# Scores of the sample tokens with the cached keys, computed during the projection of q, k, v; the norm's last addition on VectorE

## The chip, the core and the metric

The kernel runs on one core of a Trainium2 chip. The metric is the device time of one execution in microseconds. Three executions of the kernel before took 2411.53, 2411.56 and 2414.08 us; the median is 2411.56 us. One more execution was profiled, and all rows in this document's part on the kernel before come from it.

## What is computed

One decoder layer, in float32. A prompt of 4096 rows and 32 sample rows (8 sequences of 4 new tokens) go through one input projection [q | k | v | gate | lru | gate], then dilated window attention and a gated recurrence, then one output projection with a layer norm. Cut to what the change touches:

```python
q2, k2, v2, ga2, xl2, gl2 = _project(x_s, w_in)          # 32 sample rows
k_all = jnp.concatenate([ck, kh2], axis=1)               # 2048 cached keys of each sequence, and 4 new ones
v_all = jnp.concatenate([cv, vh2], axis=1)
# patterns (128,1), (512,4), (2048,16): 129 keys each, backwards from the query with stride d
idx = w_buf + jnp.arange(t)[:, None] - d * jnp.arange(N_DIL_KEYS + 1)[None, :]
s = jnp.einsum('bqhd,bqjhd->bhqj', q, jnp.take(k_all, idx, axis=1)) * (q.shape[-1] ** -0.5)
# softmax of each pattern, values, the three patterns merged by their denominators
...
z = ALPHA * x + mixed @ w_out
zn = (z - z.mean(-1)) * rsqrt(z.var(-1) + LN_EPS)
return zn * ln_g + ln_b                                  # prompt and sample rows
```

## The kernel before

Every engine runs its instructions in the order in which the program issues them, and so does SyncE's queue (SP), which issues nearly all DMAs: an instruction that waits holds up all that stand behind it on its engine.

**Phase 1** projects q, k and v. The prompt is cut into 8 tiles of 512 rows, t = 0 to 7. For t from 1 to 6 the loop runs four q groups (`qk_groups(t, 0)`), four k groups (`qk_groups(t, 1)`) and then the v stage (`v_groups(t)`); I call this a sweep. A q or k group is 24 matmuls into one PSUM bank; ScalarE copies the bank (L202) and VectorE subtracts that copy from it (L203), and SP stores both. There are six banks, used in turn (`pp`). The v stage is 8 steps (`chunk`), each of 12 matmuls, into four banks. Between its steps it prepares the input of the next sweep, one of 8 chunks per step (`next_chunk`, `prep_chunk`): VectorE transposes (L110), ScalarE rounds (L113), VectorE subtracts (L114: both inputs lie in SBUF), SP stores to DRAM. At its end SP issues the 2 MB load of the tile after next (`next_x`, L104), and the four banks are copied to `vt` tiles, of which there are three (`evac_v`, L208, two on VectorE, two on ScalarE), and stored. `sample_rows` projects the sample's v and writes the sample's q to DRAM (`qsd`); before, it stands behind the sweep t = 1.

**Phases 2 and 3** (prompt attention; recurrence and gates) aren't touched.

**Phase 4** is the output projection, in 33 blocks of 48 matmuls. A plan of times, `at(tick, f)`, sets the order: block b of the prompt starts at tick 8 b, and what belongs to it follows at fixed distances: `norm1` (VectorE, residual and statistics, L1340 to L1346; frees the block's two banks), `norm2` (VectorE, L1353), `norm3` (ScalarE, L1359), `norm4` (GpSimd, adds ln_b, L1367), `store`. `mix_split` (L1274 on ScalarE, L1275 on VectorE with two SBUF inputs) makes the left operands of the blocks to come. The sample's attention is planned into the same ticks. For each of 8 sequences: `row_q` loads its q, copied to all 128 partitions (1 MB); for each of the three patterns p = 2, 0, 1 `fetch` loads keys (256 KB for p = 2, 1 MB for the others), `k_mul` multiplies them by q on GpSimd (L1435), `k_sum` sums over the 64 columns of a head on VectorE (L1439). After four sequences `soft1` to `soft6` make the softmax, and `v_mm` multiplies with cached values on TensorE (L1492).

## Time and profile before

| | |
|---|---|
| median of three executions | 2411.56 us |
| profiled execution | 2415.58 us, span 2413.9 us (1.7 us lie around the span) |
| TensorE busy, share of the span | 93% |
| VectorE, ScalarE, GpSimd | 58%, 46%, 29% |
| sweeps t = 1 to 3 of phase 1 | about 107 to 305 us of the span |
| phase 4 | from about 1938 us to the end |
| granted TensorE clock, mean | 0.966 of full speed |

The profile gives for each engine the time in which it was busy, cuts the span into 40 slices, and names for each wait the instruction that ended it. A name such as `po<-S,mx` is output<-inputs, and L1286 is the line of the kernel.

### The profile page before, as it was taken

What the parts mean: (1) busy time and instruction counts of PE and PEld (TensorE: products, weight loads), DVE (VectorE), ACT (ScalarE), POOL (GpSimd) and SP (SyncE); (2) the same over time, 40 slices, a digit from 0 to 9 for tenths busy, and PEclk for the clock granted to TensorE, in tenths of its full rate; (3) what the DMA queues carried; (4) which work ended last, traced back from release to release, by engine and by line L of the source; (5) the groups of instructions that cost most, each with busy time, mean ns of one, the idle gap of its engine ahead of it and who ended that gap; (6) DMA issues with size and microseconds to landing.
All of it is one profiled execution on the core that took longest, in us unless ns stands there. A gap on an engine that the chain in (4) does not pass through costs nothing. (4 is left out here: it accounts for less than half of the span.)

```text
span 2413.9 us, 42627 instructions
## 1 busy us (share of the span) xinstructions
PE 2251.9 (93%) x15274; PEld 1896.7 (79%) x15274; DVE 1406.4 (58%) x3489; ACT 1099.5 (46%) x2819; POOL 695.2 (29%) x522
## 2 busy tenths in 40 slices
PE   6999999997999899989988988799999989989998
PEld 5878888886788778868777877799999967657776
DVE  4423222232476757546665655577878779998544
ACT  3212122222566566646655654566777741222221
POOL 1000000000445546464636465000000026646111
PEclk9999999998999999989999999899999989989999
DMA  6854556649666867777696755455545556668551
GB/s 174 261 189 151 173 175 200 209 186 245 181 165 174 206 155 178 182 182 172 160 211 168 182 142 134 139 174 156 168 156 178 187 183 227 244 224 325 200 187 57
DMA packets 324946, 444.18 MB, mean 184 GB/s; under 512 B 58628, under 2 KB 193412, under 8 KB 319616
## 3 DMA queue, kind: packets, MB, share of 16 engines
q1 hardware_dynamic: 324576, 440.94, 61.8%
q8 instruction: 122, 2.00, 0.4%
q14 instruction: 88, 0.72, 0.1%
q0 software_dynamic: 160, 0.52, 0.1%
HBM read 305.79 MB, written 135.60 MB: 183 GB/s over the span
## 5 line engine op out<-in xcount | busy, mean ns | idle before, releaser
L465 POOL CAST qg<-S 128x512 fp32r<-128x512 f32 x256 | 274.7, 1101 | 620.1 <-DMA S<-qd 489.7
L1286 PE MATMUL po<-S,mx 128*128 128x512 f32 x1536 | 379.9, 407 | 22.6 <-DVE xr L1340 16.8
L1286 PEld LDWEIGHTS po<-S,mx 128*128 128x128 f32 x1536 | 294.7, 194 | 113.8 <-issue 26.9
L522 DVE CUSTOM_DVE_ANT_0 sm<-s,mask 128x256 f32<-128x256 f32 (+1 forms) x768 | 270.7, 390 | 154.9 <-PE s L516 108.4
L526 ACT ACTIVATE sm<-sm,st 128x256 f32<-128x256 f32 (+1 forms) x512 | 252.9, 495 | 160.2 <-DVE st L522 133.9
L535 PE MATMUL pt<-ident,sm 128*128 128x128 f32 x1368 | 238.9, 292 | 9.4 <-ACT sm L526 9.2
L551 PE MATMUL o<-pts,v 128*64 128x128 f32 x2736 | 239.8, 292 | 6.6 <-DMA v<-vd 3.7
L539 DVE COPY pts<-pt 128x512 f32<-128x512 f32 x228 | 157.4, 690 | 142.3 <-PE pt L535 111.7
L515 PE MATMUL s<-S,qg 128*128 128x256 f32 x512 | 160.8, 334 | 51.4 <-POOL qg L465 51.0
L535 PEld LDWEIGHTS pt<-ident,sm 128*128 128x128 f32 x1368 | 145.3, 143 | 78.4 <-issue 55.3
L551 PEld LDWEIGHTS o<-pts,v 128*64 128x64 f32 x2736 | 144.7, 138 | 61.9 <-issue 4.6
L203 DVE TENSOR_TENSOR stg<-pp,stg 128x512 fp32r<-128x512 f32 x56 | 51.1, 916 | 239.0 <-ACT stg L202 239.0
L188 PE MATMUL pp<-S,xh 128*128 128x512 f32 x768 | 178.8, 393 | 6.3 <-ACT S L127 5.2
L314 PE MATMUL pp<-xh,S 128*128 128x512 f32 x448 | 176.0, 393 | 0.0
L315 PE MATMUL pp<-xh,S 128*128 128x512 f32 x448 | 174.5, 390 | 0.8 <-POOL xh L114 0.8
L188 PEld LDWEIGHTS pp<-S,xh 128*128 128x128 f32 x768 | 145.1, 189 | 38.4 <-ACT S L127 6.1
L316 PE MATMUL pp<-xh,S 128*128 128x512 f32 x448 | 174.6, 390 | 0.0
L526 ACT ACTIVATE sm<-sm,ac 128x128 f32<-128x128 f32 (+1 forms) x256 | 114.8, 450 | 103.8 <-DVE ac L522 103.2
L139 PE MATMUL xl<-xh,S 128*128 128x256 f32 x512 | 147.9, 289 | 5.0 <-DMA xh<-xtd 3.3
L653 PE MATMUL f<-xh,S 128*128 128x256 f32 x512 | 148.2, 289 | 2.6 <-DMA xh<-xtd 2.6
L143 PE MATMUL xl<-xh,S 128*128 128x256 f32 x512 | 148.2, 289 | 1.9 <-POOL S L128 1.4
L656 PE MATMUL f<-xh,S 128*128 128x256 f32 x512 | 148.2, 289 | 0.0
(287 smaller groups left out, 5303.9 us busy)
## 6 DMA issues: line engine op xcount, KB each, us to landing
xh<-xtd SPq DMA_DIRECT2D x256, 256.0 KB, 5.5
S<-qd SPq DMA_DIRECT2D x128, 256.0 KB, 5.0
xtd<-xh SPq DMA_DIRECT2D x56, 512.0 KB, 2.6
gb<-wd SPq DMA_DIRECT2D x64, 384.0 KB, 5.8
v<-vd SPq DMA_DIRECT2D x264, 64.0 KB, 4.3
S<-kd SPq DMA_DIRECT2D x64, 256.0 KB, 7.1
xr<-in_x_prompt_dram SPq DMA_DIRECT2D x32, 512.0 KB, 4.9
arena<-in_cache_k_dram SPq DMA_DIRECT2D x16, 1024.0 KB, 8.3
```

The source lines that it names most:

```text
L188: nc.tensor.matmul(p, l, m, start=(c == 0 and a + b == 0), stop=(c == 7 and (a, b) == ((1, 0) if j < 2 else (0, 1))))
L314: nc.tensor.matmul(ps, wh, xh, start=(c == 0), stop=False)
L315: nc.tensor.matmul(ps, wh, xl, start=False, stop=False)
L316: nc.tensor.matmul(ps, wl, xh, start=False, stop=(c == 7))
L465: nc.gpsimd.tensor_copy(o, q.bitcast(F32))
L515: nc.tensor.matmul(s[:, h], q_ap(x, h, 0), k, start=True, stop=False)
L522: nc.vector.tensor_tensor_reduce(x.sm[:, h, o], s[:, h, i], self.mask[:, x.pat, o], -0.125, 3e38, ALU.add, ALU.min, x.stat[:, h, 0:1])
L526: nc.scalar.activation(x.sm[:, h, o], x.sm[:, h, o], AF.Exp, bias=x.stat[:, h, 0:1], scale=-1.0, accum_out=x.stat[:, h, 1:2])
L535: nc.tensor.transpose(p[:, h, kb], x.sm[:, h, kb * 128:(kb + 1) * 128], self.ident)
L539: e(x.pt, p)
L551: nc.tensor.matmul(o[h * 64:(h + 1) * 64, x.b * 128:(x.b + 1) * 128], v[:, h * 64:(h + 1) * 64], x.pt[:, h, kb], start=(kb == kbs[0]), sto ...
L1286: self.nc.tensor.matmul(ps[j], l, self.Wo[j][c][:, s], start=(c == 0 and s == 0 and l is mh), stop=(c == 7 and l is ml))
```

## The change

Multiplications and sums of the keys are taken out of phase 4 and put into the sweeps t = 1 to 3 of phase 1. A counter of steps (`decode_step`) is called before each q and k group and after every second step of the v stage, 12 times in a sweep. A score product starts every 1.5 steps: load, multiplication one step later, sum two steps later, store of the sums to DRAM (`scd`) three steps later. The key tile `dk` is one of two buffers (pool `kfp`); the 256 KB tiles of p = 2 take a `vt` tile; q has one buffer. `sample_rows` moves ahead of t = 1. In phase 4 `scores_in` loads the sums (three DMAs of 128 KB), the softmax of the two groups stands at ticks 12 and 120, and `norm4` is on VectorE for all blocks.

```diff
+        self.scd = dr.tile([3, 128, 2 * 4 * NS], F32, name="scd")
+        dqp = xctx.enter_context(tc.tile_pool(name="p1d", bufs=1))
@@ v_groups
                 next_chunk(t, c)
+                if c % 2:
+                    decode_step()
@@ phase1
+        def row_q(b):
+            D["q"] = dqp.tile([128, NT, DA], F32, tag="q", name="qb")
+            nc.sync.dma_start(out=D["q"].rearrange("p t d -> p (t d)"),
+                              in_=dap(self.qsd, b * NT * DA, [[0, 128], [1, NT * DA]]))
+        def dec_load(b, p):
+            o = kfp.tile([128, NT, DA], F32, tag="kf", name="dk")
+            if p == 2:
+                k = sp.tile([128, DA], F32, tag="vt", name="dk2")
+                nc.sync.dma_start(out=k, in_=dap(I["cache_k"], b * 2048 * DA + 1920 * DA, [[DA, 128], [1, DA]]))
+            else:
+                a, n = ((0, 16), (1536, NT))[p]
+                k = o
+                nc.sync.dma_start(out=o, in_=dap(I["cache_k"], b * 2048 * DA + a * DA, [[n * DA, 128], [1, NT * DA]]))
+            D[b, p] = k, o
+        def dec_mul(b, p):
+            k, o = D[b, p]
+            nc.gpsimd.tensor_mul(o, k[:, None, :].to_broadcast([128, NT, DA]) if p == 2 else o, D["q"])
+        def dec_sum(b, p):
+            o = D.pop((b, p))[1]
+            D["s", b, p] = r = dqp.tile([128, NS], F32, tag="sc", name="sc", bufs=4)
+            nc.vector.tensor_reduce(r, o.rearrange("p t (h d) -> p (t h) d", d=HD), op=ALU.add, axis=AX.X)
+        def dec_save(b, p):
+            nc.sync.dma_start(out=self.scd[p, :, b * NS:(b + 1) * NS], in_=D.pop(("s", b, p)))
+        uses = [(b, p) for b in range(8) for p in (2, 0, 1)]
+        for n, (b, p) in enumerate(uses):
+            g = 1.5 * n
+            if p == 2:
+                decode.setdefault(int(g + (0.5 if b else 0)), []).append((row_q, b))
+            decode.setdefault(int(g), []).append((dec_load, b, p))
+            decode.setdefault(int(g + 1), []).append((dec_mul, b, p))
+            decode.setdefault(int(g + 2), []).append((dec_sum, b, p))
+            decode.setdefault(int(g + 3), []).append((dec_save, b, p))
+        order = {dec_sum: 0, row_q: 1, dec_load: 2, dec_mul: 3, dec_save: 4}
 ...
         def qk_groups(t, j, kp, each=None):
             for m in range(4):
+                decode_step()
                 qk_group(t, j, m)
+        sample_rows()
         for t in range(1, n_t - 1):
 ...
-            if t == 1:
-                sample_rows()
@@ phase4
         def norm4(b):
-            e = nc.gpsimd if b < n_b - 1 else nc.vector
             for w in parts(b):
-                e.tensor_add(L[b][:, w], L[b][:, w], lnb[:L[b].shape[0], w])
+                nc.vector.tensor_add(L[b][:, w], L[b][:, w], lnb[:L[b].shape[0], w])
+        def scores_in():
+            for p in range(3):
+                nc.sync.dma_start(out=SC[p].rearrange("p a b s -> p (a b s)"), in_=self.scd[p])
 ...
-        at(-17.5, row_q, 0)
+        at(-17.5, scores_in)
 ...
-    k.k_start, k.k_step, k.v_step = k.soft[9], k.soft[10], k.soft[11:]
+    k.soft_at, k.v_step = (12.0, 120.0), (24.0, 22.0)
```

VectorE's order in phase 1 from the end of the v stage t = 1 to the last k group of t = 2, before (`vt` are the copies of v, `so` those of `sample_rows`, `stg` the subtractions of the q and k groups):

```order
L208 COPY vt<-pp 128x512 x2
L349 COPY so<-pp 32x512 x2
L203 TENSOR_TENSOR stg<-pp,stg 128x512 x4
L203 TENSOR_TENSOR stg<-pp,stg 128x32x16 x4
L110 STREAM_TRANSPOSE raw<-X 128x512
```

and with the change (`sc<-dk` are the sums):

```order
L210 COPY vt<-pp 128x512 x2
L382 TENSOR_REDUCE sc<-dk 128x32
L205 TENSOR_TENSOR stg<-pp,stg 128x512 x2
L382 TENSOR_REDUCE sc<-dk 128x32
L205 TENSOR_TENSOR stg<-pp,stg 128x512
L382 TENSOR_REDUCE sc<-dk 128x32
L205 TENSOR_TENSOR stg<-pp,stg 128x512
L205 TENSOR_TENSOR stg<-pp,stg 128x32x16
L382 TENSOR_REDUCE sc<-dk 128x32
L205 TENSOR_TENSOR stg<-pp,stg 128x32x16
L382 TENSOR_REDUCE sc<-dk 128x32
L205 TENSOR_TENSOR stg<-pp,stg 128x32x16 x2
```

Between the subtractions that free the banks now stand five sums, each of which waits for GpSimd's multiplication.

SP's order at the same place, before (`X` is the 2 MB load, `vd` the store of v, `qd` that of q):

```order
L104 DMA X<-in_x_prompt_dram 32x16x256 x4
L210 DMA vd<-vt 128x512 x4
L343 DMA out_dram<-vs 32x512
L350 DMA qsd<-so 32x512
L350 DMA out_dram<-so 32x512
L192 DMA qd<-stg 128x2x512 x4
```

and with the change (`dk` are the loads of keys, `qb` that of a sequence's q, `scd` the stores of sums):

```order
L105 DMA X<-in_x_prompt_dram 32x16x256 x4
L212 DMA vd<-vt 128x512 x4
L372 DMA dk<-in_cache_k_dram 128x2048
L385 DMA scd<-sc 128x32
L194 DMA qd<-stg 128x2x512
L368 DMA dk_1561<-in_cache_k_dram 128x512
L385 DMA scd<-sc 128x32
L194 DMA qd<-stg 128x2x512
L361 DMA qb<-qsd 128x2048
L194 DMA qd<-stg 128x2x512
L372 DMA dk<-in_cache_k_dram 128x2048
L385 DMA scd<-sc 128x32
```

The loads of keys and of q now stand behind the stores of v, one by one between the stores of q.

VectorE's order in the v stage t = 2, before (`raw` and `xh` are the preparation of a chunk):

```order
L110 STREAM_TRANSPOSE raw<-X 128x512
L114 TENSOR_TENSOR xh<-raw,xh 128x2x256
L110 STREAM_TRANSPOSE raw<-X 128x512
L114 TENSOR_TENSOR xh<-raw,xh 128x2x256
L110 STREAM_TRANSPOSE raw<-X 128x512
```

and with the change:

```order
L111 STREAM_TRANSPOSE raw<-X 128x512
L115 TENSOR_TENSOR xh<-raw,xh 128x2x256
L111 STREAM_TRANSPOSE raw<-X 128x512
L115 TENSOR_TENSOR xh<-raw,xh 128x2x256
L382 TENSOR_REDUCE sc<-dk 128x32
L111 STREAM_TRANSPOSE raw<-X 128x512
```

A sum stands behind the second, the fourth and the eighth chunk.

## Rows read from the trace of the kernel before

**Rows 1.** The page: busy time of TensorE (us, share of the span, instructions), and the busy tenths of VectorE and GpSimd in 40 slices of 60 us.

```profile
PE 2251.9 (93%) x15274; PEld 1896.7 (79%) x15274; DVE 1406.4 (58%) x3489; ACT 1099.5 (46%) x2819; POOL 695.2 (29%) x522
...
DVE  4423222232476757546665655577878779998544
...
POOL 1000000000445546464636465000000026646111
```

**Rows 2.** Busy time by stretch: the early and the late part of phase 4. Columns: stretch, its length, busy us and instructions of each engine, granted clock, share of the DMA engines, GB/s.

```profile
1967.60:2160.00 192.40, 162.01 (x653) 121.54 (x654) 182.91 (x188) 40.01 (x87) 110.82 (x31) 0.91 0.62 229
2160.00:2405.80 245.80, 244.29 (x1186) 174.56 (x1185) 142.11 (x240) 51.28 (x108) 76.33 (x25) 1.00 0.56 207
```

**Rows 3.** Groups of VectorE's instructions from 1967 to 2160 us: busy us, mean ns of one, and idle time before them.

```profile
L1275 DVE SCALAR_TENSOR_TENSOR mx<-B,mx 128x256 fp32r<-128x256 f32 x28 | 42.6, 1580 | 2.1 <-ACT mx L1274 2.1
L1275 DVE SCALAR_TENSOR_TENSOR mx<-A,mx 128x256 fp32r<-128x256 f32 x26 | 40.3, 1607 | 9.4 <-ACT mx L1274 9.4
L1439 DVE TENSOR_REDUCE SC<-arena 128x32 f32<-128x2048 f32 x16 | 36.1, 2258 | 0.0
...
L1340 DVE SCALAR_TENSOR_TENSOR xr<-xr,po 128x512 f32<-128x512 f32 x28 | 17.8, 674 | 0.0
L1353 DVE SCALAR_TENSOR_TENSOR xr<-xr,mv,lng 128x1024 f32<-128x1024 f32 x13 | 16.4, 1261 | 0.0
```

**Rows 4.** The order in time of VectorE and of GpSimd around 2016 us (start, us, instruction, count).

```profile
2016.23 10.41 DVE L1275 SCALAR_TENSOR_TENSOR mx<-A,mx 128x256 fp32r<-128x256 f32 x4 [0.73 <-ACT mx L1274]
...
2016.49 9.53 POOL L1435 TENSOR_TENSOR arena<-arena,qb 128x2048 f32<-128x2048 f32 x2
```

**Rows 5.** The same line L1275 from 2000 to 2150 us, by the tile it writes: shortest, median and longest in ns.

```profile
L1275 DVE SCALAR_TENSOR_TENSOR mx<-B,mx x23: 410/416/4836, 2005.8 to 2148.4; 128x256 fp32r<-128x256 f32 x23
L1275 DVE SCALAR_TENSOR_TENSOR mx<-A,mx x20: 402/414/4835, 2016.2 to 2135.9; 128x256 fp32r<-128x256 f32 x20
```

**Rows 6.** The chain that ended last, late in phase 4: half the value products of a sequence, and a block.

```profile
2274.85 1.83 PE do L1492 x16
2276.68 11.44 PE po L1286 x48
```

**Rows 7.** TensorE's largest group from 1967.6 to 2160 us.

```profile
L1286 PE MATMUL po<-S,mx 128*128 128x512 f32 x606 | 154.5, 415 | 18.3 <-DVE xr L1340 16.2 <-DVE mx L1275 1.8
```

**Rows 8.** The order in time at the beginning of phase 4: TensorE's blocks 2 and 3 with the wait ahead of each, and ScalarE's work that stands ahead of the first.

```profile
1972.42 13.61 PE L1286 MATMUL po<-S,mx 128*128 128x512 f32 x48 [4.90 <-DVE xr L1340]
1988.79 1.56 PE L1286 MATMUL po<-S,mx 128*128 128x512 f32 x4 [2.76 <-DVE xr L1340]
...
1970.47 0.72 ACT L1274 ACTIVATE mx<-A 128x256 fp32r<-128x256 f32 x2 [10.45 <-DMA hd<-sg]
```

**Rows 9.** The granted clock (third number from the end) behind the first of these waits.

```profile
1972.00:1976.00 4.00, 3.58 (x8) 2.77 (x9) 3.29 (x9) 1.65 (x6) 0.34 (x1) 0.50 1.00 382
```

**Rows 10.** The multiplication (L1435) and the norm's last addition (L1367), over the whole span: shortest, median and longest in ns.

```profile
L1435 POOL TENSOR_TENSOR arena<-arena,qb x16: 4567/4774/5570, 1980.5 to 2217.9; 128x2048 f32<-128x2048 f32 x16
...
L1367 POOL TENSOR_TENSOR xr<-xr,lnb x31: 2337/2398/2412, 1989.4 to 2388.2; 128x1024 f32<-128x1024 f32 x31
...
L1367 DVE TENSOR_TENSOR xr<-xr,lnb x3: 692/693/1211, 2399.2 to 2410.1; 128x512 f32<-128x512 f32 x2, 32x1024 f32<-32x1024 f32 x1
```

**Rows 11.** Busy time by stretch in phase 1: the first groups of t = 1, the eight q and k groups of t = 2, its v stage. Columns as in rows 2.

```profile
101.10:107.50 6.40, 5.56 (x25) 4.17 (x24) 3.92 (x6) 2.33 (x4) 2.56 (x2) 1.00 0.97 394
...
174.20:217.90 43.70, 43.70 (x196) 36.17 (x194) 7.40 (x9) 6.62 (x9) 0.00 (x0) 1.00 0.44 137
217.90:239.80 21.90, 21.90 (x98) 18.16 (x97) 12.88 (x19) 6.69 (x10) 0.00 (x0) 1.00 0.50 201
```

**Rows 12.** VectorE and ScalarE in the v stage t = 2, in order of time: the last k group's subtraction, then the preparation of the first chunk, the start of the second, and the end of the eighth.

```profile
219.24 1.15 DVE L203 TENSOR_TENSOR stg<-pp,stg 128x512 fp32r<-128x512 f32 x1 [4.29 <-ACT stg L202]
220.30 0.70 DVE L110 STREAM_TRANSPOSE raw<-X 128x512 f32<-128x512 f32 x1
221.75 0.69 DVE L114 TENSOR_TENSOR xh<-raw,xh 128x512 fp32r<-128x512 f32 x1 [0.75 <-ACT xh L113]
222.36 0.70 DVE L110 STREAM_TRANSPOSE raw<-X 128x512 f32<-128x512 f32 x1
...
237.80 0.69 DVE L114 TENSOR_TENSOR xh<-raw,xh 128x512 fp32r<-128x512 f32 x1 [1.41 <-ACT xh L113]
```

**Rows 13.** Behind a v stage: SP's load of the next tile and stores of v (start, time from the first to the last), and the copy of the fourth bank behind the v stage t = 1 with its wait.

```profile
238.89 2.61 SPq L104 DMA_DIRECT2D X<-in_x_prompt_dram  x4
241.60 12.34 SPq L210 DMA_DIRECT2D vd<-vt  x4
...
182.09 0.59 ACT L208 COPY vt<-pp 128x512 f32<-128x512 f32 x1 [14.73 <-DMA vd<-vt]
```

**Rows 14.** The one place in phase 1 where GpSimd and VectorE work side by side, at the end of t = 0.

```profile
99.49 1.29 POOL L114 TENSOR_TENSOR xh<-raw,xh 128x512 fp32r<-128x512 f32 x1 [2.04 <-ACT xh L113]
...
100.03 1.29 DVE L114 TENSOR_TENSOR xh<-raw,xh 128x512 fp32r<-128x512 f32 x1 [0.82 <-ACT xh L113]
```

**Rows 15.** A 1 MB load with nothing of weight behind it: its issue by SP.

```profile
2326.83 0.38 SPq L1426 DMA_DIRECT2D arena<-in_cache_v_dram  x1
```

**Rows 16.** The stretches behind that issue (the share of the DMA engines is the number before the last).

```profile
2328.00:2332.00 4.00, 4.00 (x26) 1.86 (x25) 2.40 (x4) 0.00 (x0) 0.00 (x0) 1.00 0.90 313
2332.00:2336.00 4.00, 4.00 (x19) 3.22 (x18) 3.79 (x10) 1.53 (x5) 0.00 (x0) 1.00 0.02 6
```

More of the change, by code (lines that the diff above doesn't have):

```diff
@@ L350, in sample_rows, with decode_step @@
                 nc.sync.dma_start(out=dst, in_=o)
+        D, decode = {}, {}
+        def row_q(b):
[31 more added lines that the diff above has]
+        order = {dec_sum: 0, row_q: 1, dec_load: 2, dec_mul: 3, dec_save: 4}
+        tick = [0]
+        def decode_step():
+            for f, *a in sorted(decode.pop(tick[0], []), key=lambda v: order[v[0]]):
+                f(*a)
+            tick[0] += 1
         def qk_groups(t, j, kp, each=None):
             for m in range(4):
+                decode_step()
                 qk_group(t, j, m)
@@ L1377, in norm @@
                 at(t + d, f, b)
-        ck, cv = I["cache_k"], I["cache_v"]
+        cv = I["cache_v"]
         CB = 2048 * DA
@@ L1426, in fetch @@
                 nc.sync.dma_start(out=arena[s], in_=dap(src, b * CB + a * DA, [[k * DA, 128], [1, NT * DA]]))
-        def row_q(b):
-            D["q"] = qp.tile([128, NT, DA], F32, tag="X", name="qb")
-            nc.sync.dma_start(out=D["q"].rearrange("p t d -> p (t d)"),
-                              in_=dap(self.qsd, b * NT * DA, [[0, 128], [1, NT * DA]]))
-        def k_mul(n, p, s):
-            k, o, q = D.pop(n), arena[s], D["q"]
-            nc.gpsimd.tensor_mul(o, k[:, None, :].to_broadcast([128, NT, DA]) if p == 2 else o, q)
-        def k_sum(b, p, s):
-            o, sc = arena[s], SC[p][:, b // 4, b % 4]
-            nc.vector.tensor_reduce(sc, o.rearrange("p t (h d) -> p (t h) d", d=HD), op=ALU.add, axis=AX.X)
         def soft1(G):
@@ L1566, in phase4 @@
         for G in range(2):
+            for i, f in enumerate((soft1, soft2, soft3, soft4, soft5, soft6)):
+                at(self.soft_at[G] + self.soft[i], f, G)
             for i in range(4):
[L1568 to L1579 removed]
+                t0 = self.soft_at[G] + self.soft[6] + self.v_step[G] * i
                 for k, p in enumerate((2, 0, 1)):
@@ L1583, in phase4 @@
         for t, kind, b, p in sorted(uses):
-            if kind == "k" or p < 2:
+            s = None
+            if p < 2:
                 s = n % 4
```

46 lines of the change are left out of this document (14 added, 32 removed).

## The prediction

> **What bounds the kernel now.** I read the page first. TensorE is busy for 93% of the span, so only time in which it waits or runs at a low clock can be won; VectorE's slices show a 9 around 2000 us, and GpSimd is nearly empty in phase 1 [rows 1]. So I read the busy time by stretch. Early in phase 4, from 1967.6 to 2160 us, VectorE is busy for 182.9 of 192.4 us and TensorE for 162.0 at a granted clock of 0.91; later TensorE is full at 1.00 [rows 2]. The early stretch is VectorE's. Its groups say why: the 54 subtractions of L1275 take 82.9 us, 1.6 us each, and the sums 36.1 [rows 3]. In order of time four such subtractions take 10.41 us while GpSimd multiplies for 9.53 [rows 4], and by tile their median is 0.41 us and their longest 4.84 [rows 5]: most are undisturbed, some wait out a whole multiplication.
>
> In phase 1 it is the other way round: in the sweep t = 2 TensorE is busy for all of the 43.7 us of q and k groups and all of the 21.9 us of the v stage, VectorE for 7.4 and 12.9, GpSimd for nothing [rows 11]. A free engine is not yet a free place; that depends on what stands behind the moved instructions.
>
> **What phase 4 gives back.** Undisturbed, a block takes 11.44 us for 48 matmuls, 0.2383 each, and half a sequence's value products 1.83 [rows 6]. The early stretch holds 606 such matmuls [rows 7], 144.4 us, and 47 other products [rows 2]: 32 value products at 3.7 and 15 small ones, say 2. That makes 150 of 192.4 us, so 42 are lost. Not all comes back. Block 2 waits 4.90 us, and that wait goes back over VectorE to ScalarE's copies, which wait for the store of phase 3's last result [rows 8]; behind it the clock is 0.50 for 4 us, which costs 2 more [rows 9]. Block 3 waits 2.76 us, behind the first block's norm and a set of small tables on VectorE [rows 8], and again some 2 at half clock. I leave about 10 of these there and take 32 as the gain; bounds 24 (a new wait of the same kind) and 38 (both waits shrink).
>
> Does VectorE still hold TensorE up? Taken from its 182.9 us are the sums, 36.1, and the excess of 54 subtractions over 0.42, 60 [rows 3, 5]; added are 14 additions at 2 x 0.69 [rows 10], 19 us, and up to 1.2 us of waiting for ScalarE ahead of each, 17. That is 123 us in 150: hidden. Where this cover is gone an addition costs its 1.4 us per block. GpSimd's 2.40 us additions end [rows 10].
>
> The sample's 24 matmuls and transposes move ahead of t = 1, where TensorE now waits 6.40 - 5.56 = 0.84 us for the last chunks [rows 11]; they cover that: -0.9.
>
> **What phase 1 pays.** 24 multiplications of 4.77 us on GpSimd [rows 10] and 24 sums of 2.26 on VectorE [rows 3] go into three sweeps of 65.6 us. By load alone both fit: 38 us of 65.6 on GpSimd, 20.3 + 18.1 on VectorE. But the loads, the q buffer and the in-order queues form a chain, and VectorE's sums stand in it ahead of the subtractions that free TensorE's banks and ahead of the preparation of the next tile. I walk the sweep t = 2.
>
> A 1 MB load takes 4.8 us: issued at 2326.83, the DMA engines are idle from about 2331.6 [rows 15, 16]. Behind the v stage SP issues the 2 MB of the tile after next and then the stores of v; the fourth waits until ScalarE finds one of three `vt` tiles free, 14.73 us [rows 13]. Nothing was harmed by that before. Now the load of the keys of product 8 stands behind it. So from the end of the v stage: hold 14.7; load 4.8; multiplication 4.8; only now is the q buffer free, next q 4.8; multiplication 9, 4.8; sum 9, 2.3; the subtraction of one q group and its store, which stand ahead of the next load, 1.2; load 11, whose buffer sum 9 has freed, 4.8; multiplication 4.8; sum 2.3; the last two k groups' subtractions, 2 x 1.15 [rows 12]. Sum 51.6 us until VectorE starts on the next tile. Before, it starts 43.7 + 2.4 after the v stage [rows 11, 12], 46.1. It is 5.5 late, and the six banks are about used up by then.
>
> Then the v stage. A chunk takes VectorE 2.06 us from transposition to transposition [rows 12], eight 16.5; three sums add 6.8; and the subtraction of L114 has two SBUF inputs, as L1275 has. Beside a GpSimd instruction it took 1.29 us instead of 0.69 and ended with that instruction [rows 14]. A multiplication met in this stage costs 4.77 less what transposition and rounding cover, 1.4: 3.4. By the order of the loads two fall into the stage in the first two sweeps and three in the third, 23.5 in all. The q and k groups' subtractions read PSUM and one SBUF tile, as L1340, which stays at 0.67 beside the multiplications [rows 3]; I charge them nothing.
>
> The Trainium skill, "SBUF — State Buffer", section "Who interferes with whom", has it that the engine that starts first keeps the shared port for its whole instruction and the other "fully blocks", and that tensor_reduce never contends. By that rule the meetings cost the 23.5 just taken. Read as a proportional slowing instead, from the mean of 1.59 us against 0.42 [rows 3, 5], each of 24 subtractions would grow by 1.9 us, 46 in all, and the forecast by 22. The median beside the longest [rows 5] agrees with the rule; the sums stay at 2.26 us [rows 3].
>
> Three sweeps: 3 x (51.6 + 16.5 + 6.8) + 23.5 = 248 us, where 3 x 65.6 = 197 are there: 51 late. At the end of a v stage there is slack: the eighth chunk is ready at 238.5 [rows 12], and TensorE, done at 239.8, comes to it after seven chunks of three matmuls, 4.8 us later: 6.1. So TensorE loses 45. Bounds: 22, if no subtraction is held up (51 - 23.5 - 6), and 65, if loads take 7 us, as three of them stand in each sweep's chain.
>
> **The sum.** 45 - 32 - 0.9 = +12 us. On the profiled execution's 2415.6 that is 2428; that execution is 4 us above the median, so 2424 for a median. This measurement tells a change from none at about 0.2%, 5 us.
>
> **Rivals.**
> 1. *All of phase 1 is hidden.* For it: six banks take 27 us of lateness from the q and k groups, and TensorE is the only bound there. Then 2411.6 - 33 = 2379. It decides if a sweep's chain falls from 51.6 to below 46 and the v stage to below 24.3 (18.2 and the slack); without the hold of 14.7 it would nearly. Chance 0.08.
> 2. *Only the v stage pays.* The q and k groups stay in time, the v stage takes 16.5 + 6.8 + 6.8 = 30.1 against 24.3 twice, and 33.5 once: 21 us. 21 - 33 = -12, 2400: faster. It decides if the hold is at most 9 us, since then VectorE starts in time. Chance 0.20.
> 3. *The loads are late too.* The moved transfers are 26 MB in 197 us; at the 382 GB/s that full DMA engines moved [rows 9] that is 68 us, a share of 0.35, on top of 0.44 and 0.50 [rows 11]. If loads take 8 us because they meet stores and the tile load, 3 sweeps x 3 loads x 3.2 = 29 more: 2453. Chance 0.11.
> 4. *Phase 4 gives back only 20*, because `norm4` waits for ScalarE ahead of the norm that frees the banks: 2436. Against it stands the room of 27 us above. Chance 0.06.
>
> The forecast itself has 0.55. The range of 2394 to 2452 holds it, the fourth rival, most of the second and about half of the third. Its own range is 2412 to 2442. Faster by over 0.2%: all of the first, 0.16 of the second and 0.02 of the forecast's lower end, 0.26. Within 0.2%: 0.09. Slower: 0.65.
>
> **What would show it.** In the changed profile the v stages t = 1, 2, 3 should end late by about 15 us more each time; TensorE should wait for VectorE's L115 at the start of the q groups of t = 2, 3, 4, and for a bank ahead of the v stages; VectorE should wait for GpSimd's multiplication at L382, and some subtractions of L115 should take up to 5 us. SP should stand for some 14 us behind each tile load, the keys behind it. In phase 4 L1327 should be at 0.42 us throughout, and TensorE without waits behind block 3. Wrong would be the forecast if the sums find their products ready (then the first or second rival), or if TensorE still waits in phase 4.

## The result, and the profile after

The changed kernel takes **2439.44 us** (median of 4 runs, 2435.91 to 2444.75), against 2411.55 for the kernel before on the same chip: a ratio of 1.0115, 95% interval 1.0095 to 1.0135. It is slower by 27.9 us, where I had forecast 12. The sign is as forecast and the time lies within the range, but the size is more than twice the forecast's.

The profiled execution took 2439.8 us (span 2438.1), 24.2 more than that of before. From its page, as in [rows 1], with the granted clock by slices of 61 us in addition:

```profile
PE 2259.7 (93%) x15274; PEld 1891.3 (78%) x15274; DVE 1387.9 (57%) x3520; ACT 1094.5 (45%) x2819; POOL 618.8 (25%) x491
...
DVE  4354653222257666664755566467888786455555
...
POOL 1044350000145464745544566300000000000000
PEclk9998889999899999999999999799999998999999
```

GpSimd's work has moved from the end to the third to sixth slice, and from the fourth to the sixth the clock is down as well. The windows tell what each stretch gained or lost (length, busy us and instructions of each engine, clock, DMA share, GB/s): phase 1; phases 2 and 3; phase 4. First before, then after.

```profile
0.00:573.60 573.60, 552.15 (x2591) 459.10 (x2592) 179.71 (x278) 136.12 (x214) 13.57 (x21) 0.99 0.60 194
573.60:1937.60 1364.00, 1267.22 (x10746) 1121.11 (x10745) 875.13 (x2737) 854.65 (x2378) 489.61 (x430) 0.96 0.65 172
1937.60:2413.90 476.30, 432.54 (x1942) 316.53 (x1940) 351.59 (x477) 108.73 (x228) 192.04 (x71) 0.95 0.57 208
```

```profile
0.00:632.60 632.60, 577.67 (x2591) 467.16 (x2592) 258.33 (x302) 135.79 (x215) 124.09 (x45) 0.95 0.68 220
632.60:1986.30 1353.70, 1258.05 (x10747) 1112.96 (x10745) 876.51 (x2734) 849.96 (x2376) 489.66 (x430) 0.97 0.65 173
1986.30:2438.10 451.80, 423.94 (x1942) 311.22 (x1940) 253.05 (x485) 108.74 (x229) 5.01 (x16) 0.97 0.45 159
```

Phase 1 lost **59.0 us** (forecast: 45 - 0.9), phase 4 gave back **24.5** (forecast: 32). Phases 2 and 3, which the change does not touch, are 10.3 us shorter in this execution: the same matmuls (10746 and 10747 in the rows) were busy for 9.2 us less, at a clock of 0.97 and not 0.96. In the profiled executions of the experiments that stretch takes 1354 to 1365 us, so I count it as variation between executions. 59.0 - 24.5 - 10.3 is the 24.2 of the two profiled executions; without the 10.3 it would be 34.5, where the medians are 27.9 apart. No run assigns that rest.

Of phase 1's 59.0 us TensorE waited 33.5 more, and 25.5 are the same 2591 matmuls taking longer at the lower clock.

**Phase 1, sweep t = 2.** The same places as in [rows 12, 13]: SP's queue, then GpSimd, then VectorE (start, duration, instruction, wait ahead of it).

```profile
194.37 2.60 SPq L105 DMA_DIRECT2D X<-in_x_prompt_dram  x4
197.07 13.15 SPq L212 DMA_DIRECT2D vd<-vt  x4
210.31 0.38 SPq L372 DMA_DIRECT2D dk<-in_cache_k_dram  x1
...
221.10 0.32 SPq L361 DMA_DIRECT2D qb<-qsd  x1
...
233.90 0.41 SPq L372 DMA_DIRECT2D dk<-in_cache_k_dram  x1
...
216.47 4.61 POOL L377 TENSOR_TENSOR dk<-dk,qb 128x2048 f32<-128x2048 f32 x1 [23.05 <-DMA dk<-in_cache_k_dram]
225.88 4.60 POOL L377 TENSOR_TENSOR dk<-dk,qb 128x2048 f32<-128x2048 f32 x1 [4.80 <-DMA qb<-qsd]
...
240.57 4.57 POOL L377 TENSOR_TENSOR dk<-dk,qb 128x2048 f32<-128x2048 f32 x1 [3.51 <-DMA dk<-in_cache_k_dram]
...
210.39 1.29 DVE L205 TENSOR_TENSOR stg<-pp,stg 128x512 fp32r<-128x512 f32 x2 [10.84 <-ACT stg L204]
...
249.48 0.70 DVE L111 STREAM_TRANSPOSE raw<-X 128x512 f32<-128x512 f32 x1
```

From the issue of the tile's load at 194.37 to VectorE's first transposition at 249.48 the chain takes 55.1 us. In brackets stands what I had put: hold (from the issue of the tile's load until the stores of v are out of SP's queue and the first load of keys is issued) 15.9 (14.7), load 6.2 (4.8), multiplication 4.6 (4.8), row of q 4.8 (4.8), multiplication 4.6 (4.8), sum, subtraction and store 3.4 (3.5), load 6.7 (4.8), multiplication 4.6 (4.8), sum and two subtractions 4.3 (4.6). The order was right; both loads were longer. The first row of VectorE shows that the hold has a second way: ScalarE, too, waits for a store of v, and VectorE behind ScalarE.

Then the v stage: three subtractions of L115 that met a multiplication, the multiplications beside them, and the undisturbed subtraction of the eighth chunk.

```profile
250.86 4.71 DVE L115 TENSOR_TENSOR xh<-raw,xh 128x512 fp32r<-128x512 f32 x1 [0.69 <-ACT xh L114]
256.93 4.85 DVE L115 TENSOR_TENSOR xh<-raw,xh 128x512 fp32r<-128x512 f32 x1 [0.73 <-ACT xh L114]
275.99 3.92 DVE L115 TENSOR_TENSOR xh<-raw,xh 128x512 fp32r<-128x512 f32 x1 [0.73 <-ACT xh L114]
281.26 0.69 DVE L115 TENSOR_TENSOR xh<-raw,xh 128x512 fp32r<-128x512 f32 x1 [0.73 <-ACT xh L114]
...
250.43 4.60 POOL L377 TENSOR_TENSOR dk<-dk,qb 128x2048 f32<-128x2048 f32 x1 [5.28 <-DMA dk<-in_cache_k_dram]
256.63 4.61 POOL L377 TENSOR_TENSOR dk<-dk,qb 128x2048 f32<-128x2048 f32 x1 [1.60 <-DMA dk<-in_cache_k_dram]
274.85 4.52 POOL L377 TENSOR_TENSOR dk<-dk,qb 128x2048 f32<-128x2048 f32 x1 [13.61 <-DMA dk<-in_cache_k_dram]
```

Each of the three ends 0.54 us after the multiplication that it met. They cost 4.0 + 4.2 + 3.2 = 11.4 us; I had put two at 3.4. I had read [rows 14] as a subtraction that ends with GpSimd's instruction; its rows, too, put the end 0.54 us later (101.32 against 100.78). The waits between 95 and 420 us (engine, line, what it waited for; us in total, times, longest) name the same links:

```profile
POOL dk L377 <- DMA dk<-in_cache_k_dram: 120.2, 17, 23.0
...
DVE sc L382 <- POOL dk L377: 77.5, 14, 10.6
...
ACT vt L210 <- DMA vd<-vt: 54.2, 3, 19.8
```

and TensorE's groups on the page show at which places this reached it (busy us, mean ns, idle before):

```profile
L190 PE MATMUL pp<-S,xh 128*128 128x512 f32 x768 | 184.2, 401 | 15.3 <-DVE stg L205 9.1
L317 PE MATMUL pp<-xh,S 128*128 128x512 f32 x448 | 181.3, 405 | 13.5 <-DVE xh L115 13.5
L316 PE MATMUL pp<-xh,S 128*128 128x512 f32 x448 | 182.8, 408 | 11.5 <-ACT xh L114 10.6
```

**Phase 4.** VectorE's subtractions are as forecast: from 2016 to 2209 us none is longer than 0.43 us, where [rows 5] has 4.84.

```profile
L1327 DVE SCALAR_TENSOR_TENSOR mx<-B,mx x31: 415/418/427, 2022.1 to 2208.9; 128x256 fp32r<-128x256 f32 x31
```

But TensorE has a new place to wait, in the stead of the waits of [rows 8]: the transposes of the scores (TensorE, then ScalarE, then the first 50 us of phase 4).

```profile
2023.52 0.69 PE L1490 MATMUL ds<-ident,SC 128*128 128x128 f32 x2 [7.01 <-ACT fo L1558]
2027.00 0.47 PE L1490 MATMUL ds<-ident,SC 128*128 128x128 f32 x1 [2.79 <-DVE SC L1484]
...
2017.61 0.72 ACT L1326 ACTIVATE mx<-A 128x256 fp32r<-128x256 f32 x2 [8.34 <-DMA hd<-sg]
...
2022.91 0.56 ACT L1558 COPY fo<-pf 12x512 f32<-12x512 f32 x1
...
1986.30:2036.30 50.00, 35.93 (x140) 28.26 (x139) 36.32 (x79) 23.53 (x49) 5.01 (x16) 0.80 0.51 166
```

ScalarE waits for the last store of phase 3 as before; what stands behind it now is the copy that frees the bank of the transposes, and the plan has no block between that they could wait under. Behind them TensorE runs at a granted clock of 0.50 until 2032 us.

A second new place stands all along the stretch behind (TensorE's waits from 2016 to 2440 us: us in total, times, longest):

```profile
PE pa L1545 <- DVE om L1539: 4.1, 5, 0.8
```

`pa` are the matmuls that follow a sequence's value products, `om` is VectorE's product in between. In the kernel before, a block lay between the last value product and `pa` (2274.85 to 2287.96 us, for one), and none of these matmuls waited. The new times of the value products (`soft_at`, `v_step`) put `pa` right behind them in five of the eight sequences, and each time TensorE waits 0.81 us.

### The profile page after: what moved, and what is told of

It is laid out like the page before. It is cut to its first block, busy times and chain, and to the rows that moved or that the text cites. A ratio compares the mean times of both kernels' runs of the same rounds, so it can differ in the third digit from the quotient of the medians.

```text
span 2438.1 us, 42645 instructions
## 1 busy us (share of the span) xinstructions
PE 2259.7 (93%) x15274; PEld 1891.3 (78%) x15274; DVE 1387.9 (57%) x3520; ACT 1094.5 (45%) x2819; POOL 618.8 (25%) x491
## 4 chain that ended last, share of the span: by engine, by line
PE 60%; DMA 15%; POOL 9%; DVE 5%; SPq 4%; issue 4%; ACT 2%; POOLq 0%; ACTq 0%; DVEq 0%
PE po L1338 15%; PE pp L190 5%; POOL gb L850 4%; PE pt L587 4%; PE o L603 4%; DMA gb<-wd 4%; POOL qg L517 2%; PE pg L1016 2%; PE pg L1018 2%; PE pg L1017 2%; PE xl L140 2%; PE xl L144 2%; PE xl L142 2%; PE pp L316 2%; PE pp L317 2%
## 5 line engine op out<-in xcount | busy, mean ns | idle before, releaser
L1338 PE MATMUL po<-S,mx 128*128 128x512 f32 x1536 | 371.5, 401 | 4.8 <-DVE S L129 4.3
L587 PEld LDWEIGHTS pt<-ident,sm 128*128 128x128 f32 x1368 | 145.1, 143 | 76.9 <-issue 55.6
L190 PE MATMUL pp<-S,xh 128*128 128x512 f32 x768 | 184.2, 401 | 15.3 <-DVE stg L205 9.1
L317 PE MATMUL pp<-xh,S 128*128 128x512 f32 x448 | 181.3, 405 | 13.5 <-DVE xh L115 13.5
L316 PE MATMUL pp<-xh,S 128*128 128x512 f32 x448 | 182.8, 408 | 11.5 <-ACT xh L114 10.6
L318 PE MATMUL pp<-xh,S 128*128 128x512 f32 x448 | 178.9, 399 | 0.0
L377 POOL TENSOR_TENSOR dk<-dk,qb 128x2048 f32<-128x2048 f32 x24 | 110.5, 4606 | 157.5 <-DMA dk<-in_cache_k_dram 120.2
```

Source lines behind the costliest of these rows:

```text
L190: nc.tensor.matmul(p, l, m, start=(c == 0 and a + b == 0), stop=(c == 7 and (a, b) == ((1, 0) if j < 2 else (0, 1))))
L316: nc.tensor.matmul(ps, wh, xh, start=(c == 0), stop=False)
L317: nc.tensor.matmul(ps, wh, xl, start=False, stop=False)
L318: nc.tensor.matmul(ps, wl, xh, start=False, stop=(c == 7))
L587: nc.tensor.transpose(p[:, h, kb], x.sm[:, h, kb * 128:(kb + 1) * 128], self.ident)
L1338: self.nc.tensor.matmul(ps[j], l, self.Wo[j][c][:, s], start=(c == 0 and s == 0 and l is mh), stop=(c == 7 and l is ml))
```

## The experiments

Every kernel here is the changed kernel with the edit shown, cut to what matters (`...`). Ratios are to the kernel before on the same chip; "at 2411.6" is the ratio times 2411.6. The table has, from VectorE's rows, the **v stages** of t = 1, 2, 3 (first transposition to the end of the eighth subtraction), behind each the **gap** to the next tile's first transposition, and how much later than before phase 1 ends. (The first gap of the kernel before holds the sample's rows as well.)

| run | v | gap | v | gap | v | gap | phase 1 |
|---|---|---|---|---|---|---|---|
| before | 18.2 | 53.5 | 18.2 | 47.1 | 18.2 | 47.1 | 0 |
| changed | 31.4 | 55.5 | 32.5 | 55.4 | 30.2 | 42.3 | +59.0 |
| e1_no_keys | 18.2 | 47.1 | 18.2 | 47.1 | 18.2 | 47.1 | -1.4 |
| e5_norm4_pool | 31.4 | 55.8 | 32.5 | 55.1 | 30.3 | 42.1 | +60.6 |
| e14_soft_later | 27.4 | 55.8 | 29.1 | 56.3 | 29.8 | 43.1 | +53.3 |
| e2_no_mul | 20.9 | 45.7 | 21.1 | 44.5 | 20.8 | 42.9 | -0.8 |
| e7_no_port | 21.6 | 57.1 | 23.0 | 55.2 | 26.8 | 41.9 | +37.8 |
| e8_hi_psum | 21.2 | 57.2 | 22.5 | 53.5 | 26.8 | 42.8 | +37.9 |
| e12_split_mul | 24.9 | 57.2 | 26.3 | 54.9 | 28.9 | 42.8 | +47.3 |
| e9_pool_queue | 33.8 | 54.1 | 28.0 | 47.8 | 36.9 | 42.5 | +58.6 |
| e4_spread_x | 31.9 | 50.9 | 32.6 | 50.9 | 30.1 | 42.7 | +50.5 |
| e15_late_x | 31.8 | 50.3 | 32.3 | 58.0 | 27.9 | 43.1 | +55.5 |
| e19_no_x | 31.2 | 45.5 | 28.5 | 47.3 | 31.9 | 42.3 | +39.6 |
| e16_hp_late_x | 21.3 | 55.6 | 22.3 | 56.6 | 27.1 | 41.2 | +37.5 |
| e17_all | 21.2 | 54.7 | 22.5 | 55.2 | 25.5 | 43.1 | +33.2 |
| e20_x_pool_q | 21.1 | 51.3 | 23.0 | 52.2 | 26.2 | 42.5 | +30.3 |
| e21_x_act_q | 21.3 | 53.7 | 23.0 | 51.2 | 27.6 | 42.8 | +32.5 |
| e22_halves | 21.3 | 49.0 | 22.6 | 53.1 | 25.2 | 41.2 | +27.1 |
| e23_all_late | 21.2 | 55.3 | 22.2 | 50.7 | 24.9 | 42.1 | +20.8 |

TensorE alone sets 47.1 us for a gap behind a v stage of 18.2, and less behind a longer one (44.5 and 45.7 in e2_no_mul); a v stage may take 18.2 and the slack of about 5. Behind the third v stage hardly any key work is left. e5 and e14 leave phase 1 as it is and end it 60.6 and 53.3 us late: one execution with meetings in it varies by some 7 us, and for small differences the timed ratios decide.

### Is it the key work, and which part of it?

`uses = []` and a table of zeros stored in place of the scores:

> The changed kernel without any key work in the projections: no loads of keys, no rows of q, no multiplications and no sums; the table of scores is stored as zeros, so the scores of the sample tokens against the cached keys are left out. Theory (phase 1 lost about 59 us to the key work, phase 4 gained about 31): 2411.6 - 31 - 1 = about 2379 us, with the eighth chunk of each tile back at the times of the kernel before. Rival A (the norm's addition on VectorE costs something beside the gain, or phase 4 gains only through other changes): 2385 to 2400. Rival B (a good part of the loss in phase 1 comes from the move of the sample rows or from stores, not from the key work): above 2395.

Measured: 0.9885 (0.9869 to 0.9902), 2383.9 at 2411.6; phase 1 ends 1.4 us earlier than before, phase 4 takes 24.6 us less. So all of phase 1's loss is key work (the move of the sample's rows gave the 0.9 I had put for it, or a little more), and phase 4's 24.5 is its full gain. The 5 us above my 2379 are phase 4's, for which I had put 31.

```
 def dec_mul(b, p):
-    nc.gpsimd.tensor_mul(o, ...)
+    pass
 ...                                # the sums read the keys as loaded
```

> GpSimd's 24 multiplications left out; loads, rows of q, sums and saves stay in their places, the sums read the keys as loaded. Theory (the loss is a serial chain of hold, load, multiplication and sum, in which VectorE stands, plus the meetings of the subtraction with the multiplication): a sweep is hold 14.7 + load 6 + sum 2.3 + load 6 + sum 2.3 = 31 to the end of the groups of q and k, + v stage 23.4 = 55 us, less than TensorE's 65 us, so nothing of it shows: 2380 to 2386 us. Rival A (VectorE's sums, 2.3 us each, are what costs: 24 x 2.3 = 55 us): stays near 2435. Rival B (the loads and the held SyncE are enough by themselves, the multiplication only shares the wait): 2400 to 2420.

Measured: 0.9874 (0.9858 to 0.9891), 2381.2; phase 1 -0.8. All loads, rows of q and sums are there, and cost nothing. The sums alone are not the loss (rival A), nor is the held queue (rival B); it needs the multiplication, which stands in the chain and in the subtractions' way.

### The meetings in the v stage

```
-    (lo or nc.vector).tensor_sub(lo_, r, hi.bitcast(F32))
+    nc.vector.tensor_sub(lo_, hi.bitcast(F32), z)          # z: zeros in PSUM; from tile 1 on
 ...
```

> From tile 1 on VectorE's subtraction that makes the low part of a chunk reads the rounded chunk from SBUF and zeros from PSUM, in place of two operands from SBUF: the same elements and the same waits for ACT, but one SBUF operand (the low part is wrong by that, and with it what is computed). Theory (meetings with a running multiplication cost 3.4 us each, three per v stage, beside a chain of loads that stays): phase 1 gives back 3 x 10 = 30 us at most, what remains is the hold and the chain: 2410 to 2422 us. Rival A (the meetings are the whole loss): 2380 to 2390. Rival B (meetings are hidden in the chain, VectorE would wait for the same multiplication at the sum anyway): 2432 to 2440.

```
+    nc.scalar.copy(h, r)          # h in PSUM; from tile 1 on
+    nc.vector.tensor_sub(lo_, r, h.bitcast(F32))
     nc.scalar.copy(hi, r)
-    (lo or nc.vector).tensor_sub(lo_, r, hi.bitcast(F32))
 ...
```

> The changed kernel; from tile 1 on ScalarE writes the rounded chunk twice, first to PSUM, then to SBUF; VectorE's subtraction reads the one in PSUM, so it has one operand in SBUF, and computes the same. Theory (the run with a zeroed PSUM operand showed 20 us for these meetings): v stages of 22 to 27 us in place of 30 to 32.5, 2419 to 2424 us. Rival A (ScalarE's additional 0.62 us per chunk comes into the way, eight times per tile): 2430 to 2440. Rival B (one PSUM operand is no protection, and the other run was faster because its operands were ready earlier): 2436 to 2444.

Measured: 1.0036 (1.0024 to 1.0047) and 1.0039 (1.0028 to 1.0051), both 2420 to 2421. The v stages fall by 3 to 10 us each and phase 1 by 21, the gaps hardly change. In the second of the two kernels the subtraction keeps its 0.69 us in the middle of a multiplication (VectorE, then GpSimd):

```profile
244.43 0.69 DVE L117 TENSOR_TENSOR xh<-raw,hp 128x512 fp32r<-128x512 f32 x1 [0.66 <-ACT hp L116]
...
243.98 4.62 POOL L383 TENSOR_TENSOR dk<-dk,qb 128x2048 f32<-128x2048 f32 x1 [5.22 <-DMA dk<-in_cache_k_dram]
```

So the meetings cost some 20 us of the 59 (21 of phase 1, 18 to 19 by the timed ratios), near the 23.5 of my sum; ScalarE's second copy costs nothing that the two ratios could tell.

```
-    nc.gpsimd.tensor_mul(o, ...)
+    for n in range(4):
+        nc.gpsimd.tensor_mul(o[:, n], k if p == 2 else o[:, n], D["q"][:, n])
```

> Each of GpSimd's multiplications is cut into four of a quarter of the size, back to back. Theory (a subtraction waits for the instruction that runs, so for at most a quarter): a meeting costs up to 1.2 us in place of 3.4, v stages of 25 to 27 us in place of 30 to 32.5, 2422 to 2428 us. Rival A (GpSimd's next piece starts before VectorE gets its turn, so a subtraction waits for all four): 2438 to 2444. Rival B (four instructions take longer than one, each with a fixed cost): the multiplications of 4.6 us grow to 5.5 or more and the chain by 4 us a sweep, 2440 to 2450.

Measured: 1.0081 (1.0064 to 1.0098), 2431, between theory and rivals, since both are true in part. The longest subtraction falls from 4.92 to 1.76 us (shortest, median, longest in ns, from 160 to 360 us):

```profile
L115 DVE TENSOR_TENSOR xh<-raw,xh x24: 691/1088/1758, 164.7 to 354.7; 128x512 fp32r<-128x512 f32 x24
```

but more of them meet a piece (the median is 1.09 and not 0.69), and four pieces take 5.0 to 6.0 us in place of 4.6. VectorE does get its turn between the pieces. This is what the Trainium skill has in "SBUF — State Buffer", section "Who interferes with whom": the lock is held for one instruction, and the other side waits for its end; the 0.5 us from the end of a multiplication to that of the subtraction above, and the 1.76 here, agree with it.

### The gap

```
-    nc.sync.dma_start(out=o, ...)          # loads of keys, and the row of q
+    nc.gpsimd.dma_start(out=o, ...)
```

> The loads of keys and the rows of q are issued by GpSimd in place of SyncE, at the same places of the program. Theory (SyncE's order is the chain: the first load of a sweep stands behind the stores of v, the others behind the stores of the q and k groups): from the end of a v stage to the next tile's first transposition VectorE takes TensorE's 47 us in place of 55.5, twice; the v stages stay at 30 to 32.5: 2411.6 + 27.9 - 17 = about 2422 us. Rival A (the 2 MB of the tile takes its share of the DMA engines wherever it stands, as with the load cut in four): 2430 to 2436. Rival B (issuing from GpSimd costs it time, or its order makes the multiplications wait for buffers): 2440 to 2460.

Measured: 1.0139 (1.0124 to 1.0154), 2445: slower. SP's order is not all of it. GpSimd stood 17 us with the 256 KB load of a p = 2 tile (L368), and the multiplication behind it in its order waited as long, though its keys had been issued at 202.91 us (GpSimd, then ScalarE):

```profile
220.58 0.54 POOL L368 DMA_DIRECT2D dk<-in_cache_k_dram  x1 [17.09 <-ACT stg L204]
221.13 4.63 POOL L377 TENSOR_TENSOR dk<-dk,qb 128x2048 f32<-128x2048 f32 x1
...
219.48 0.59 ACT L210 COPY vt<-pp 128x512 f32<-128x512 f32 x1 [19.31 <-DMA vd<-vt]
```

That load goes into one of the three `vt` tiles, and those hold v until its stores, which stand behind the tile's 2 MB, are done: ScalarE's copy into a `vt` tile waited 19.31 us for such a store and began 1.1 us before the load got out. So with SP out of the chain the hold most likely reaches it through the `vt` tiles; the releaser that the row names, a copy of a q group, is the profile's inference, and no run gave the load a buffer of its own.

The next two move the tile's 2 MB: in four pieces, one ahead of each q group; and whole, ahead of the fourth q group.

```
     def v_groups(t):
-        next_x(t)
+        late.append(t)
     def qk_groups(t, j, kp):
+        if j == 0 and m == 3 and late: next_x(late.pop())
```

> The next tile's 2 MB load is cut into four pieces of 0.5 MB that are issued at the next four groups of q, in place of the whole load ahead of the four stores of v; all else as in the changed kernel. Theory (chain with the hold of 14.7 us in it, three times): a sweep falls from 55.1 + 32.5 = 87.6 to about 73 us against TensorE's 65.6; phase 1 loses 3 x 7.3 - 5 = about 17 in place of 59: about 2397 us (2385 to 2410). Rival A (meetings of GpSimd and VectorE are the main loss): the hold gives its slack only, 2430 to 2440. Rival B (the traffic of the load itself delays the key loads wherever it stands): 2415 to 2430.

> The next tile's 2 MB load is issued as a whole, but ahead of the last group of q of the next sweep in place of ahead of the stores of v. Theory (the hold of 16 us goes, and the load runs while GpSimd multiplies or VectorE sums): from the end of a v stage to the next tile's first transposition 47 to 48 us in place of 55.5, twice; about 2422 us. Rival A (its traffic delays the next row of q or the next keys by as much, as with four pieces): 2429 to 2434. Rival B (the tile comes too late for the next v stage): above 2440.

Measured: 1.0081 (1.0055 to 1.0107), 2431, and 1.0103 (1.0077 to 1.0130), 2436. My theory fell in both, and the second can't be told from the changed kernel: the hold shrank from 16 to about 6 us, but most came back at another link. With four pieces the row of q takes 9.8 us (SP, GpSimd):

```profile
210.62 0.32 SPq L363 DMA_DIRECT2D qb<-qsd  x1
...
220.39 4.61 POOL L379 TENSOR_TENSOR dk<-dk,qb 128x2048 f32<-128x2048 f32 x1 [9.79 <-DMA qb<-qsd]
```

and with the whole load later, a load of keys 11.6:

```profile
216.41 3.40 SPq L105 DMA_DIRECT2D X<-in_x_prompt_dram  x4
...
224.50 0.42 SPq L374 DMA_DIRECT2D dk<-in_cache_k_dram  x1
...
236.13 4.61 POOL L379 TENSOR_TENSOR dk<-dk,qb 128x2048 f32<-128x2048 f32 x1 [8.34 <-DMA dk<-in_cache_k_dram]
```

Is it the tile's load at all? Tiles 3 to 5 are not loaded:

> The changed kernel without the 2 MB loads of the tiles 3, 4 and 5: their v stages prepare tile 2 again, so the projections of these tiles are wrong; all else stays. Theory (the tile's transfer costs the key chain its time wherever it stands: as a hold of 16 us ahead of it, or as longer rows of q and keys): without it the chain is 6 + 5 + 4.6 + 4.8 + 4.6 + 2.3 + 1.1 + 5 + 4.6 + 2.3 + 2.1 = 42 us, less than TensorE's 47, so S = 47 in place of 55.5, twice: about 2422 us, with loads of 4.8 us. Rival A (the loads are long through the stores of q, k, v and of the transposed input): 6 us and more also here, 2428 to 2432. Rival B (the chain is paced by something else, TensorE's half clock behind the v stage or GpSimd): 2436 to 2440.

Measured: 1.0036 (1.0015 to 1.0057), 2420; gaps (S in the text above) of 45.5 and 47.3, TensorE's own time. So the tile's load is the cause of the long gaps, as a hold ahead of the chain or as traffic within it: this run takes away both, and where the two runs before took away most of the hold, the gaps fell by 5 us at most. But the loads of keys did not come down to 4.8:

```profile
200.98 0.38 SPq L375 DMA_DIRECT2D dk<-in_cache_k_dram  x1
...
224.95 0.41 SPq L375 DMA_DIRECT2D dk<-in_cache_k_dram  x1
...
207.32 4.60 POOL L380 TENSOR_TENSOR dk<-dk,qb 128x2048 f32<-128x2048 f32 x1 [12.85 <-DMA dk<-in_cache_k_dram]
...
231.59 4.62 POOL L380 TENSOR_TENSOR dk<-dk,qb 128x2048 f32<-128x2048 f32 x1 [2.86 <-DMA dk<-in_cache_k_dram]
```

6.3 and 6.6 us from issue to the start of the work. Half of rival A is true: a load of keys takes longer than 4.8 us also with no tile's load beside it. What I had read in [rows 16] was the end of the transfer, not the moment from which its reader may start. The Trainium skill, "DMA: Bandwidth & Descriptors", section "Anatomy of one DMA — SWDGE (gpsimd) path", puts a fixed cost of about 2 us beside the transfer, most of it between the data's arrival and the signal. It says so of DMAs that GpSimd issues; the 1.5 to 1.8 us here, on SyncE's queue, are near it, but the row of q, 1 MB as well, took 4.8 us from issue to reader in the changed kernel (221.10 to 225.88). So how much of the 1.5 to 1.8 is the signal, and how much the stores of q, k and v that still run or the keys' own transfer, no run separates.

### Phase 4

The norm's addition back on GpSimd:

> The changed kernel with the norm's addition back on GpSimd (all but the last block), all else as changed. Theory (with the multiplications gone from phase 4 neither engine is the bound there; VectorE is busy for half of it): no difference, 2437 to 2442 us. Rival A (GpSimd's additions of 2.4 us still hold up VectorE's subtractions L1327, and through them TensorE): 2445 to 2455. Rival B (VectorE's waits for ScalarE ahead of the addition delay the block): faster, 2430 to 2435.

Measured: 1.0102 (1.0076 to 1.0127), 2436: no difference that the intervals could tell. The moved addition is hidden, as forecast, on either engine.

```
-    k.soft_at, k.v_step = (12.0, 120.0), (24.0, 22.0)
+    k.soft_at, k.v_step = (20.0, 128.0), (24.0, 22.0)
```

> Phase 4 alone: the softmax over the scores and the value products behind it are planned 8 units, one block of output rows, later (20 and 128 in place of 12 and 120). Theory (phase 4 gives back 25 and not 32 us because the transposes of the scores now stand where TensorE waits 7.0 us for ScalarE's copy of the last states, and 2.8 us for the scores, and runs 13.7 us at half clock behind): these waits go, 6 to 12 us: 2428 to 2434 us. Rival A (the wait goes back to ScalarE's wait for the last store of phase 3 and appears at the next block in any order, as 4.9 and 2.8 us before the change): 2436 to 2440. Rival B (the value products come too late for the end): 2442 to 2455.

Measured: 1.0086 (1.0068 to 1.0104), 2432. The 7 us less than the changed kernel are within the two intervals; phase 4 in its trace takes 447.3 us in place of 451.8, 446 to 447 also in the runs below that have this edit. The 7.0 us wait is gone, block 2's of 4.55 is back, the 2.8 us wait for the scores stays (2.70), and the clock of the first 50 us is 0.93 and not 0.80:

```profile
2024.41 13.01 PE L1338 MATMUL po<-S,mx 128*128 128x512 f32 x48 [4.55 <-DVE xr L1392]
...
1991.90:2041.90 50.00, 39.58 (x164) 31.12 (x163) 36.96 (x79) 21.77 (x46) 5.01 (x16) 0.93 0.52 169
```

### Together

> The later load of the tile together with the rounded chunk in PSUM for VectorE's subtraction. Theory (two separate losses of phase 1, the meetings and the chain, that add up): 20 + 16 us less than the changed kernel: about 2404 us, faster than the kernel before. Rival A (the later load gives 8 us as the four pieces did): 2411 to 2413. Rival B (one loss hides the other, the chain sets the pace): 2418 to 2421 as with the PSUM operand alone.

> Both of these and the softmax one block later. Theory (three separate losses): about 2396 us, faster than the kernel before by 0.6 per cent. Rival A (the softmax gives nothing): as the run without it, about 2404. Rival B (neither the later load nor the softmax gives anything): 2418 to 2421.

Measured: 1.0033 (1.0018 to 1.0049) and 1.0015 (1.0004 to 1.0027). Both theories fell: the later load gives nothing beside the PSUM operand (1.0033 against 1.0039 without it). The later softmax adds its some 4 us, which shows in phase 4's trace; the two intervals overlap. Three places for the tile's load, each with the PSUM operand and the later softmax:

> Rounded chunk in PSUM for the subtraction, softmax one block later, and the tile's load issued by GpSimd at its old place, in place of SyncE. Theory (in another queue it shares the DMA engines with the key loads and does not stand ahead of them): no hold, loads of 7 to 10 us: 2400 to 2408. Rival (its traffic takes the same time from the chain as in SyncE's queue): 2414 to 2418 as with the later load.

> As the run before, but the tile's load is issued by ScalarE. Theory: 2400 to 2408. Rival (ScalarE waits with the issue until VectorE has done with the old tile, and its copies of v with it): 2412 to 2420.

> Rounded chunk in PSUM, softmax one block later, and the tile's load in two halves, one issued behind the row of q, one behind the load of keys at the first k group, where the DMA engines wait for GpSimd and VectorE anyway. Theory (the transfer fits into the time in which the chain multiplies and sums): 47 to 49 us from v stage to the next tile, 2394 to 2402 us, faster than the kernel before. Rival (it meets a load there too): 2412 to 2418.

Measured: 0.9992 (0.9977 to 1.0007), 0.9992 (0.9980 to 1.0005) and 0.9980 (0.9964 to 0.9996), or 2410, 2410 and 2407 at 2411.6: each between its theory and its rival. Another engine's queue takes 1 to 4 us off a gap, no more; two halves behind the loads of the chain take 5.7 off the first and 2.1 off the second. In the third sweep the first half still stood ahead of a load of keys. The last run moves the places of the halves:

```
-    next_x(0)                      # ahead of the sample's rows
+    late = [2]
 ...
+    if late and (j, m) in ((0, 3 if t == 2 else 1), (1, 0)):
+        x_half(j)
 ...                                # the PSUM operand in the three sweeps with key work alone
```

> As the run with two halves; in addition the load of tile 2 is also taken from ahead of the first sweep (there the rows of the sample's q stood 13.7 us behind it), the halves of the first and third sweep are issued at the second group of q and the first of k, where no row of q or keys is issued behind them, and the rounded chunk goes to PSUM in the three sweeps with key work alone. Theory (each place where the tile's transfer stands ahead of a link of the chain costs its time): 8 us less in the first sweep, 6 in the third, 3 ahead of the first: about 2396 us, a ratio of 0.993 to the kernel before. Rival (the chain is now paced by its own loads, multiplications and sums in each sweep): as the run with two halves, 0.998.

Measured: 2402.1 beside 2418.1 for the kernel before, a ratio of **0.9934** (0.9912 to 0.9957), 2395.7 at 2411.6. Phase 1 still loses 20.8 us, phase 4 takes 446.4; what is left of phase 1's loss no run takes apart. The first sweep's v stage starts at 155.4 us and not at 165.6 as with the halves alone, near the 11 that I had put for it. The second sweep's gap, 55.3 us, is longer by 6 than with the halves alone, which I did not expect. Most of it stands in one load of keys, behind the first half: 13.2 us from issue to reader (209.75 to 222.97) in place of 8.9 (218.07 to 226.94). Why it took longer, no run shows.

## Why the prediction was right in sign and wrong in size

- **What bounds each stage, and that the sign is set by a sum of two stages:** right. Both rivals that ended on the other side asked for a hold that is shorter or not there; it was 15.9 us.
- **Phase 4 gives back 32: failed in size, 24.5.** "I leave about 10 of these there" is the step. I kept the waits of [rows 8] as they stood and put no other. But with the scores ready the change moved the transposes of the scores forward, to where TensorE has no block, behind the same ScalarE wait: 7.0 + 2.8 us and half clock behind them. The later softmax shows 4.5 of the missing 7.5 us. And the new times of the value products brought the five waits of L1545, 4.1 us, which stand in that run too. The two cover the 7.5 within what two executions differ by. The bound of 24 ("a new wait of the same kind") was this case.
- **`norm4` hidden, GpSimd's meetings gone in phase 4, sample rows -0.9:** right.
- **Phase 1 pays 45: failed in size, 59 to 60.** The walk of the sweep was right in every link and its order. The step that failed is the price of its links, "A 1 MB load takes 4.8 us" above all. Against the run without keys the eighth subtraction is 22.2, 44.9 and 65.2 us late at t = 1, 2, 3; I had 16.1, 32.2 and 51.7. In the sweep t = 2, of 6.6 us too few: the two 1 MB loads +3.3 ("a 1 MB load takes 4.8 us": 6.2 to 6.7), the hold +1.2, other links -1.0; the v stage +2.4 (three meetings of 3.2 to 4.2 in place of two at 3.4, for a subtraction ends 0.54 us behind the multiplication and not with it; but two sums within it and not three); +0.4 from the end of the v stage to the load's issue; and 0.3 because a sweep of TensorE's own is 65.3, not 65.6. The first sweep stood behind a tile's load as well, through the sample's rows (VectorE's second copy of them waited 14.09 us for a store of v), which I had not walked. The slack is 5 and not 6.1.
- **The third rival, loads late too,** is half true: +1.4 to 1.9 us per load of keys in the sweep t = 2, not 3.2, and most of it (1.5 to 1.8) also without the tile's load. My own bound "if loads take 7 us" was 65. The page of the kernel before had a row that I did not use, the loads of keys themselves from issue to landing (KB, median us); the changed kernel's is below it:

```profile
arena<-in_cache_k_dram SPq DMA_DIRECT2D x16, 1024.0 KB, 8.3
dk<-in_cache_k_dram SPq DMA_DIRECT2D x16, 1024.0 KB, 5.9
```

- **The signs to look for:** v stages late by 20 to 23 us each time (forecast "about 15"); waits for L115, for banks, at L382, subtractions up to 4.92 us, SP's 13 us behind the tile's load of this sweep: all there. "TensorE without waits behind block 3" failed: the 7.0 and 2.8 us stand ahead of it, but the five of L1545 behind it.
- **By the rule of the Trainium skill ("SBUF — State Buffer", "Who interferes with whom") the meetings cost 23.5, by a proportional reading 46:** 18 to 21 measured.
- TensorE's lower clock in phase 1 (0.95 on the mean, 0.54 from 194 to 200 us behind the first v stage) was no step of mine. In the gaps VectorE is later than TensorE, so I take most of its 25.5 us as time in which TensorE would have waited otherwise; no run separates it.
- Both errors in size went the same way and added up, to 34.5 in place of 12. That 27.9 lies nearer to the forecast is no merit of it: it is the rest that no run assigns.
